# Conv/NSA hybrid decoder step on one core: the compression of the cached blocks in wider and fewer matrix products

## The chip, the cores and the metric

The kernel runs on one core of a Trainium2 chip. The metric is device time in microseconds (us) for one execution; a kernel's time is the median of its runs.

## The reference, cut to what matters

The reference is one inference step of a two-layer decoder, for a prompt of 256 new tokens and for 8 sequences with 4 new tokens each and 2048 cached positions. Nearly all of its arithmetic is in four feed-forward blocks and in the projections of a short convolution and of a sparse attention. The part that the change touches is the compressed branch of the attention: the cached keys and values of each sequence are cut into blocks of 32 positions, and each block is turned into one key and one value by a small two-layer network.

```python
def compress(rows, pe, w1k, w2k, w1v, w2v):
    B, T = rows.shape[:2]
    blk = rows.reshape(B, T // L_CMP, L_CMP, 2, N_KV_HEADS, HEAD_DIM) + pe[:, None, None, :]
    k = jax.nn.gelu(jnp.einsum('bnlkd,lde->bnke', blk[:, :, :, 0], w1k)) @ w2k
    v = jax.nn.gelu(jnp.einsum('bnlkd,lde->bnke', blk[:, :, :, 1], w1v)) @ w2v
    return k, v
```

Here L_CMP is 32, there are 4 key/value heads of 64, and a sequence's 2048 cached positions lie in 16 pages of 128 positions, so in 64 blocks.

## The kernel before, in words

The activations stand with features on the 128 partitions and the 288 tokens (256 + 32) in the free dimension. The large products run as three passes in a rounded 32-bit format: each weight chunk is loaded into a `raw` buffer (four buffers, SyncE's queue, SP), ScalarE (ACT) writes its high part `whi`, VectorE (DVE) its low part `wlo` (lines 227 and 236), and TensorE (PE) multiplies high by high, high by low and low by high, each with 288 columns, all through the helper `mm` (line 292). PE thus runs through the program's products one after the other, and ACT, DVE and POOL prepare weights and take results away beside it.

The compression does not depend on the new tokens. It is written as a generator, `cmp_side` (lines 727 to 799), and `tick` (line 482) takes a step of it now and then while the first three feed-forward blocks and the convolution are put into the program; each `yield` says how much of that work must pass before the next step. So the compression's products stand between the large ones, in PE's one order.

Its work comes in 16 pieces, two for each of the 8 sequences. A piece is 8 whole pages (a `cp` tile of 128 x 8 x 512, two buffers); the page's 512 columns are 2 (key or value) x 16 steps x 16 (4 blocks x 4 heads), and the partitions hold two positions of 64 features. For each of the 16 steps, and for keys and values, one product of a 128 x 64 weight with 128 columns is added into the hidden tile `H` (lines 784 to 786): 32 products, the key's into partitions 0 to 63 and the value's into 64 to 127. They are in plain float32, which PE runs as two instructions each. `gelu_hidden` (line 703) and `gelu_hidden2` (line 711) put the activation on H with ACT, DVE and POOL. `second` (lines 768 to 777) applies the second layer to the hidden tile of the piece before, right behind a piece's 32 products: two products for the keys (weights `W2`, 64 columns each), four for the values (the hidden tile as 64 x 32 weights, `W2` as 64 columns), and two copies out, into `KcT` (DVE) and `Vc` (ACT). In the trace these read as `acc<-cp,W`, `acc<-Hs,W` and `acc<-W,Hs`.

Pages are loaded through SP two pieces ahead, in four groups of two pages for a piece (`load`, line 735): a group reads its page numbers and then gives out one transfer of 256 KB for each page. The weight loads use the same queue, in the order of the program.

Behind these stages come the attention, whose order a planner of costs and ranks (class `Plan`) sets, the output projection and the last feed-forward block. At the planner's end three weight preparations for the output projection (`EARLY`, lines 1485 to 1488) have a rank of about 100; all other ranks lie between -57 and 37, and a lower rank goes first.

Of the kernel before, what the change touches and what calls it, by code (L numbers as in the profile page):

```python
# [8 lines left out]
F32 = mybir.dt.float32  # L9
F32R = mybir.dt.float32r  # L10
I32 = mybir.dt.int32
AF = mybir.ActivationFunctionType
# [4 lines left out]
P = 128  # L17
# [5 lines left out]
NB = 8  # L23
NT = 4
NS = NB * NT
N = NP + NS
KV = 4
# [233 lines left out]
def tile_step(ctx, tc, x_turned, vectors, state_turned, cmp_pages, sel_pages, cache_win, win_pages, page_table,  # L261
# [3 lines left out]
    nc = tc.nc  # L265
# [19 lines left out]
    def trb():  # L285
        return bank("tr")

    def accb():
        return bank("acc")

    def mm(out, lhsT, rhs, start, stop):
        nc.tensor.matmul(out, lhsT, rhs, start=start, stop=stop, skip_group_check=True)  # L292
# [4 lines left out]
    ffn0 = work.enter_context(tc.tile_pool(name="ffn0", bufs=2))  # L297
    pti = const.tile([1, NB * 16], I32, name="pti")
    sT = ffn0.tile([P, KD, 16], F32, name="sT", bufs=1)
    W2 = const.tile([P, HD], F32, name="W2")  # L300
# [20 lines left out]
    def tr(out, in_):  # L321
# [4 lines left out]
    W = Weights(nc, raw, split, RAW, dict(  # L326
        w_ffa_gu=w_ffa_gu, w_ffa_down=w_ffa_down, w_ffb_gu=w_ffb_gu, w_ffb_down=w_ffb_down, w_conv_in=w_conv_in,
        w_conv_out=w_conv_out, w_nsa_in=w_nsa_in, w_nsa_out=w_nsa_out))
# [32 lines left out]
    for _ in range(4):  # L361
        c = W.chunk()
# [47 lines left out]
    def begin(pg, pu):  # L410

        nc.scalar.activation(root, eps, AF.Sqrt)
        warm = accb()
        for n in range(WARM):
            mm(warm[:, :P], ones, ones, True, True)

        def filler(n):
            for _ in range(n):
                mm(warm[:, :P], ones, ones, True, True)

        W.convert()
        for d in range(KD):
            gated_hi(d, V_FFA)
        for d in range(KD):
            gated_lo(d, V_FFA)
        hi, lo = W.take()
        steps = FIRST.split()
        for n, step in enumerate(steps):
            if step == ".":
                filler(2)  # L430
                continue
            k = int(step[1])
            w, x = (lo if step[0] == "l" else hi), (xl if step[0] == "x" else xh)
            mm(pg[:, :N], w[:, k], x[:, k], n == 0, n == len(steps) - 1)
        W.convert()

        sq = []
        room = ffn0.tile([P, 8, 512], F32, name="cp").rearrange("p a c -> p (a c)")[:, :9 * N].rearrange("p (d c) -> p d c", c=N)
        for d in range(0, KD, 3):
            n = min(3, KD - d)  # L440
            sq.append(room[:, d:d + n])
            nc.scalar.activation(sq[-1], xT[:, d:d + n], AF.Square)
            if len(sq) == 1:
                W.convert()
        hi, lo = W.take()
        for w, xs in ((hi, (xh, xl)), (lo, (xh,))):
            for k in range(KD):
                for x in xs:
                    mm(pu[:, :N], w[:, k], x[:, k], k == 0 and w is hi and x is xh, k == KD - 1 and w is lo)
        nc.vector.tensor_add(sq[0], sq[0], sq[1])  # L450
        nc.vector.tensor_add(sq[0][:, :2], sq[0][:, :2], sq[2])
        nc.vector.tensor_add(ss, sq[0][:, 0], sq[0][:, 1])
        nc.vector.tensor_add(ss, ss, sq[0][:, 2])
        load_rest()
# [245 lines left out]
    KcT = mid.tile([P, 2, NB, 64], F32, name="KcT")  # L700
    Vc = mid.tile([P, NB, KV * HD], F32, name="Vc")
    b1 = const.tile([P, 1], F32, name="b1")
    def gelu_hidden(H, w, pool):
        x, x2 = [pool.tile([P, P], F32, name=n)[:, :w] for n in ("Hx", "Hs")]
        nc.scalar.activation(x if len(H.shape) == 2 else x.rearrange("e (k g n) -> e k g n", k=H.shape[1], g=H.shape[2]), H, AF.Identity, bias=b1)
        nc.scalar.activation(x2, x, AF.Square)
        nc.vector.tensor_scalar(x2, x2, 0.044715, 1.0, op0=OP.mult, op1=OP.add)
        nc.gpsimd.tensor_mul(x2, x2, x)
        return x, x2
# [11 lines left out]
    def page_numbers(n, k):  # L721

        return nc.values_load_multi_w_load_instructions(
            pti[0:1, n:n + k], engines=(mybir.EngineType.SP,), min_val=0, max_val=sel_pages.shape[0] - 1,
            skip_runtime_bounds_check_because="the page table's entries are pages of the caches")[1]

    def cmp_side(cw):

        yield WAITS[0] * FILL
        W1 = load_w1(cw)  # L730
        nc.scalar.dma_start(W2, w_cmp2)
        yield WAITS[1] * FILL
        tiles = {}

        def load(n, j):

            if n < 2 * NB:
                if j == 0:
                    tiles[n] = cw.tile([P, 8, 512], F32, name="cp")
                for k, at_ in enumerate(page_numbers(n * 8 + j * 2, 2)):  # L740
                    nc.sync.dma_start(tiles[n][:, j * 2 + k:j * 2 + k + 1], cmp_pages[bass.ds(at_, 1)].rearrange("s p c -> p s c"))

        for n in range(2):
            for j in range(4):
                load(n, j)
                yield WAITS[2] * FILL

        part = []
        for h in range(2):
            t = [cw.tile([P, N], F32, name=x) for x in ("t1", "t2", "s1", "a")]  # L750
            part.append(cw.tile([P, P], F32, name="Hx" if h else "Hs"))
            for q in range(4):
                v = t[q][:, :256].rearrange("p (s e) -> p s e", s=2)
                s0 = 8 * h + 2 * q
                nc.gpsimd.tensor_tensor(v, W1[:, s0:s0 + 2], vecT[:, V_PE + s0:V_PE + s0 + 2, None].to_broadcast([P, 2, P]), op=OP.mult)
                if q:
                    nc.gpsimd.tensor_add(t[0][:, :256], t[0][:, :256], t[q][:, :256])  # L757
            yield WAITS[3] * FILL
            nc.gpsimd.tensor_add(part[h], t[0][:, :P], t[0][:, P:256])
        nc.gpsimd.tensor_add(part[0], part[0], part[1])  # L760
        yield WAITS[3] * FILL
        pb = accb()
        mm(pb[:, 0:1], part[0], ones[:, 0:1], True, True)
        nc.vector.tensor_scalar(b1, pb[:, 0:1], float(D), None, op0=OP.mult)
        yield 0.3

        def second_of(Hs, b, h):
            def second():
                z = accb()
                for kp in range(2):  # L770
                    mm(z[kp * 64:(kp + 1) * 64, 0:64], W2[0:64],
                       Hs[0:64].rearrange("e (pr kp n) -> e kp pr n", pr=2, kp=2)[:, kp], True, True)
                hs = slice(h * 32, (h + 1) * 32)
                for kv in range(KV):
                    mm(z[hs, 64 + kv * 64:128 + kv * 64], Hs[64:, kv * 32:(kv + 1) * 32], W2[64:], True, True)
                nc.vector.tensor_copy(KcT[:, :, b, hs], z[:, 0:64].rearrange("p (a n) -> p a n", a=2))
                nc.scalar.activation(Vc[hs, b], z[hs, 64:320], AF.Copy)
            return second

        second = None  # L780
        for n in range(2 * NB):
            H = accb()
            v = tiles.pop(n).rearrange("p g (c a x) -> p c a g x", c=2, a=16)
            for st in range(16):
                for c in range(2):
                    mm(H[c * 64:(c + 1) * 64, :P], W1[:, st, c * 64:(c + 1) * 64], v[:, c, st], st == 0, st == 15)
            if second:
                second()
            for j in range(4):
                yield 1.15  # L790
                if j == 0:

                    hidden = gelu_hidden(H[:, :P].rearrange("e (g k n) -> e k g n", g=8, k=KV), P, cw)
                load(n + 2, j)
                if j == 2:
                    gelu_hidden2(*hidden)
            second = second_of(hidden[1], *divmod(n, 2))
        second()
        yield 0.6


    def nsa(at):
# [14 lines left out]
        W1 = load_w1(tin)  # L817
# [162 lines left out]
        order = [(i, j, b2) for i, j in chunks for b2 in range(2)]  # L980
        pages, rings = {}, {}
        room = {"raw": 0, "early": 0, "split": 0}
# [103 lines left out]
        for u in range(KD):  # L1086
            pr, g = divmod(u, 4)
            p = mmb()
# [27 lines left out]
        def step(engine, name, put, after=(), slots=(), uses=(), rank=0.0):  # L1116
            return plan.add(engine, TAKES[name], put, after, slots, uses, rank)
# [365 lines left out]
            prompt_unit(*unit)  # L1483
        before = values_of[:PAGES["until"] // 2]
        for n, engine in enumerate(EARLY):
            before = [step("ACT", "whi", W.high, [*before, loads[len(order) + n // 2]], rank=100.0 + n)]
            lower = {"POOL": nc.gpsimd, "DVE": nc.vector}[engine]
            step(engine, "wlo" if engine == "POOL" else "wlo_v", lambda n=W.done + n, lower=lower: W.low(n, lower), before, rank=100.5 + n)

        room["split"] = PAGES["split"]  # L1490
        load_more(0.0)
# [108 lines left out]
```

## Time and profile before

| | us |
|---|---|
| median of 3 runs (1264.59 to 1267.12) | 1266.42 |
| time of the profiled execution | 1265.62 |
| its span, first to last instruction | 1263.5 |
| PE busy in the span | 1242.1 (98%) |
| DVE busy | 719.9 (57%) |
| ACT busy | 582.8 (46%) |
| POOL busy | 250.3 (20%) |
| compression, first layer, PE busy (`acc<-cp,W`) | 59.4 |
| DMA, mean | 207 GB/s |

The span is 2.1 us shorter than the profiled execution's own time, and that time is 0.8 us under the median. In the rows below, PE is the matrix product and PEld the load of its weights; a name such as `acc<-cp,W` is the tile written and the tiles read; `128*64 128x128` is the weight (rows * columns) and the moving operand (partitions x columns). Several products of one kind that run in one another's wake are merged into one row of the timeline: the time from its start to the next row's start is what the group took of PE's time, while the duration of one product holds the filling and emptying of the array too, and so is longer than the distance from one to the next.

### The profile page before, as it was taken

Reading aid. Unit: us, or ns where it says so; the run is one execution under the profiler, and the core shown is the slowest. Engines: PE = TensorE matmul, PEld = TensorE weight load, DVE = VectorE, ACT = ScalarE, POOL = GpSimd, SP = SyncE. Lnnn points to the kernel's source line nnn. Section 1 sums busy time; section 2 is a strip of 40 time slices with the busy share of each in tenths; the row PEclk is TensorE's granted clock in tenths of the full one; section 3 lists DMA queues with packets and bytes.
Section 4 is the critical chain, followed back from the end, with each engine's and each line's share of the span. In section 5 each row is a group of like instructions: output and inputs, shape, how many; then the busy total and the mean of one; then the engine's idle time right before and its main releaser. Section 6 shows DMA issues by size and latency. Waiting matters only on the chain.

```text
span 1263.5 us, 26708 instructions
## 1 busy us (share of the span) xinstructions
PE 1242.1 (98%) x10679; PEld 1193.5 (94%) x10679; DVE 719.9 (57%) x1377; ACT 582.8 (46%) x1054; POOL 250.3 (20%) x261
## 2 busy tenths in 40 slices
PE   9999999999999999999999999999999999999997
PEld 8999999999989999999999999999866599999997
DVE  6653455666655445556464456576568666644553
ACT  6443344533453334345444344544288655443444
POOL 0260121222212101112121022130022122210211
PEclk9999999999999999999999999999999999999999
DMA  7754645656546456546563544487799857565432
GB/s 274 267 199 174 229 162 190 250 184 214 187 159 226 168 202 222 199 155 216 211 227 124 184 144 141 152 302 232 231 359 332 297 213 267 214 249 200 157 104 78
DMA packets 71565, 262.06 MB, mean 207 GB/s; under 512 B 7953, under 2 KB 9874, under 8 KB 56210
## 3 DMA queue, kind: packets, MB, share of 16 engines
q1 hardware_dynamic: 70418, 249.66, 55.7%
q0 software_dynamic: 256, 8.32, 1.7%
q10 hardware_dynamic: 768, 2.38, 0.5%
q8 instruction: 84, 1.38, 0.4%
q14 instruction: 39, 0.32, 0.1%
HBM read 257.31 MB, written 11.35 MB: 213 GB/s over the span
## 4 chain that ended last, share of the span: by engine, by line
PE 88%; ACT 4%; DVE 3%; DMA 2%; POOL 1%; issue 1%; SPq 1%; ACTq 0%; DVEq 0%; POOLq 0%
PE mm L292 78%; PE acc L292 8%; PE tr L323 2%; ACT whi L227 1%; DVE wlo L236 1%; ACT S L1199 1%; SPq L997 1%; ACT L523 1%; DMA early<-in_sel_pages_dram 0%; POOL t L757 0%; DMA raw<-in_w_nsa_out_dram 0%; POOL a L538 0%; ACT sq L385 0%; DMA wlo<-in_sel_pages_dram 0%; DMA raw<-in_w_ffa_gu_dram 0%
## 5 line engine op out<-in xcount | busy, mean ns | idle before, releaser
L292 PE MATMUL mm<-xh,whi 128*128 128x288 f32 x1832 | 544.9, 299 | 3.0 <-DVE xl L1464 1.6
L292 PE MATMUL mm<-xh,wlo 128*128 128x288 f32 x1832 | 540.0, 297 | 0.7 <-DVE wlo L236 0.7
L292 PE MATMUL mm<-xl,whi 128*128 128x288 f32 x1832 | 533.2, 293 | 0.0
L236 DVE TENSOR_TENSOR wlo<-raw,whi 128x1024 fp32r<-128x1024 f32 (+2 forms) x361 | 406.4, 1139 | 120.5 <-ACT whi L227 117.7
L227 ACT ACTIVATE whi<-raw 128x1024 fp32r<-128x1024 f32 (+2 forms) x365 | 343.1, 953 | 90.1 <-PE mm L292 81.2
L292 PEld LDWEIGHTS mm<-xh,whi 128*128 128x128 f32 x1832 | 344.4, 189 | 6.2 <-issue 1.9
L292 PEld LDWEIGHTS mm<-xl,whi 128*128 128x128 f32 x1832 | 346.8, 190 | 0.5 <-DVE xl L379 0.2
L292 PEld LDWEIGHTS mm<-xh,wlo 128*128 128x128 f32 x1832 | 341.9, 187 | 1.8 <-DVE wlo L236 1.6
L292 PE MATMUL mm<-Ah,wlo 128*128 128x288 f32 x768 | 228.5, 297 | 1.7 <-DVE wlo L236 1.7
L292 PE MATMUL mm<-Ah,whi 128*128 128x288 f32 x768 | 228.1, 297 | 1.5 <-ACT Ah L541 1.0
L292 PE MATMUL mm<-Al,whi 128*128 128x288 f32 x768 | 227.3, 296 | 0.4 <-DVE Al L542 0.4
L538 POOL TENSOR_TENSOR a<-s,t 128x288 f32<-128x288 f32 x88 | 115.1, 1307 | 492.6 <-DVE t L536 322.2
L292 PEld LDWEIGHTS mm<-Ah,whi 128*128 128x128 f32 x768 | 145.1, 189 | 2.4 <-ACT Ah L541 1.2
L292 PEld LDWEIGHTS mm<-Ah,wlo 128*128 128x128 f32 x768 | 144.1, 188 | 3.1 <-DVE wlo L236 3.1
L292 PEld LDWEIGHTS mm<-Al,whi 128*128 128x128 f32 x768 | 144.5, 188 | 0.6 <-DVE Al L542 0.6
L541 ACT ACTIVATE Ah<-a 128x288 fp32r<-128x288 f32 x88 | 39.2, 445 | 143.9 <-POOL a L538 143.7
L534 ACT ACTIVATE s<-t 128x288 f32<-128x288 f32 x88 | 39.2, 445 | 141.9 <-DVE t L532 141.7
L536 DVE TENSOR_TENSOR t<-mm,rB 128x288 f32<-128x288 f32 x88 | 40.2, 456 | 90.6 <-PE mm L292 90.5
L542 DVE TENSOR_TENSOR Al<-a,Ah 128x288 fp32r<-128x288 f32 x88 | 40.7, 462 | 68.6 <-ACT Ah L541 68.6
L572 DVE SCALAR_TENSOR_TENSOR xT<-mm,xT 128x288 f32<-128x288 f32 x64 | 29.2, 457 | 83.3 <-PE mm L292 83.2
L292 PE MATMUL acc<-cp,W 128*64 128x128 f32 x1024 | 59.4, 274 | 0.0
L292 PEld LDWEIGHTS acc<-cp,W 128*64 128x64 f32 x1024 | 55.6, 137 | 2.8 <-issue 2.8
(282 smaller groups left out, 870.4 us busy)
## 6 DMA issues: line engine op xcount, KB each, us to landing
raw<-in_w_ffb_gu_dram SPq DMA_DIRECT2D x44, 1024.0 KB
raw<-in_w_ffa_gu_dram SPq DMA_DIRECT2D x42, 1024.0 KB
cp<-in_cmp_pages_dram SPq DMA_DIRECT2D x128, 256.0 KB
early<-in_sel_pages_dram SPq DMA_DIRECT2D x56, 256.0 KB
raw<-in_w_ffa_down_dram SPq DMA_DIRECT2D x16, 768.0 KB
raw<-in_w_conv_in_dram SPq DMA_DIRECT2D x12, 1024.0 KB
raw<-in_w_ffb_down_dram SPq DMA_DIRECT2D x16, 768.0 KB
raw<-in_sel_pages_dram SPq DMA_DIRECT2D x48, 256.0 KB
```

What stands on the lines that cost most here:

```text
L227: self.nc.scalar.activation(parts[0], v, AF.Copy)
L236: (lower or self.nc.vector).tensor_sub(parts[1], v, parts[0])
L292: nc.tensor.matmul(out, lhsT, rhs, start=start, stop=stop, skip_group_check=True)
L323: nc.tensor.transpose(out, in_, ident[:k, :k])
L523: nc.scalar.activation(root, eps, AF.Sqrt)
L534: nc.scalar.activation(s1, t1, AF.Silu)
L536: nc.vector.tensor_mul(t2, pu[:, :N], rB)
L538: nc.gpsimd.tensor_mul(a, s1, t2)
L541: nc.scalar.activation(Ah[:, f], a, AF.Copy)
L542: nc.vector.tensor_sub(Al[:, f], a, Ah[:, f])
L572: nc.vector.scalar_tensor_tensor(xT[:, d], py[:, :N], 0.5, xT[:, d], op0=OP.mult, op1=OP.add)
L997: nc.sync.dma_start(v[:, s:s + 1], sel_pages[bass.ds(at_[s0 + s], 1)].rearrange("s p c -> p s c"))
```

## The change

A piece is now half the steps of all 16 pages of a sequence, where it was all steps of half the pages. The cache's columns are laid out so (16 steps, then key or value) that a page's two halves of 256 columns are 8 steps each; the layout is made outside the timed program, as before. A piece's products are 16, with 256 columns each, and a sequence's two pieces add into the same H, which now comes from the bank ring `tr` and not `acc`. The activation and the second layer run once a sequence, on 256 hidden columns. A page group is now four half pages, each a transfer of 128 KB whose rows are 1 KB. The ranks of the `EARLY` preparations go from about 100 to about 1000.

```diff
-    def gelu_hidden(H, w, pool):
-        x, x2 = [pool.tile([P, P], F32, name=n)[:, :w] for n in ("Hx", "Hs")]
+    def gelu_hidden(H, w, pool, **k):
+        x, x2 = [pool.tile([P, w], F32, name=n, **k) for n in ("Hx", "Hs")]
...
             if n < 2 * NB:
+                b, h = divmod(n, 2)
                 if j == 0:
-                    tiles[n] = cw.tile([P, 8, 512], F32, name="cp")
-                for k, at_ in enumerate(page_numbers(n * 8 + j * 2, 2)):
-                    nc.sync.dma_start(tiles[n][:, j * 2 + k:j * 2 + k + 1], cmp_pages[bass.ds(at_, 1)].rearrange("s p c -> p s c"))
+                    tiles[n] = cw.tile([P, 16, 256], F32, name="cp")
+                for k, at_ in enumerate(page_numbers(b * 16 + j * 4, 4)):
+                    nc.sync.dma_start(tiles[n][:, j * 4 + k:j * 4 + k + 1],
+                                      cmp_pages[bass.ds(at_, 1), :, h * 256:(h + 1) * 256].rearrange("s p c -> p s c"))
...
-        def second_of(Hs, b, h):
-            def second():
-                z = accb()
-                for kp in range(2):
-                    mm(z[kp * 64:(kp + 1) * 64, 0:64], W2[0:64],
-                       Hs[0:64].rearrange("e (pr kp n) -> e kp pr n", pr=2, kp=2)[:, kp], True, True)
-                hs = slice(h * 32, (h + 1) * 32)
-                for kv in range(KV):
-                    mm(z[hs, 64 + kv * 64:128 + kv * 64], Hs[64:, kv * 32:(kv + 1) * 32], W2[64:], True, True)
-                nc.vector.tensor_copy(KcT[:, :, b, hs], z[:, 0:64].rearrange("p (a n) -> p a n", a=2))
-                nc.scalar.activation(Vc[hs, b], z[hs, 64:320], AF.Copy)
-            return second
-
-        second = None
+        def second(Hs, b):
+            z, y = accb(), accb()
+            for kp in range(2):
+                mm(z[kp * 64:(kp + 1) * 64, 0:P], W2[0:64], Hs[0:64].rearrange("e (pr kp n) -> e kp pr n", pr=2, kp=2)[:, kp], True, True)
+            for kv in range(KV):
+                mm(y[0:64, kv * 64:(kv + 1) * 64], Hs[64:, kv * 64:(kv + 1) * 64], W2[64:], True, True)
+            nc.vector.tensor_copy(KcT[:, :, b], z[:, 0:P].rearrange("p (a n) -> p a n", a=2))
+            nc.scalar.activation(Vc[0:64, b], y[0:64, :256], AF.Copy)
+
+        hidden = None
         for n in range(2 * NB):
-            H = accb()
-            v = tiles.pop(n).rearrange("p g (c a x) -> p c a g x", c=2, a=16)
-            for st in range(16):
+            b, h = divmod(n, 2)
+            if h == 0:
+                H = trb()
+            v = tiles.pop(n).rearrange("p g (a c x) -> p a c g x", c=2, a=8)
+            for st in range(8):
                 for c in range(2):
-                    mm(H[c * 64:(c + 1) * 64, :P], W1[:, st, c * 64:(c + 1) * 64], v[:, c, st], st == 0, st == 15)
-            if second:
-                second()
+                    mm(H[c * 64:(c + 1) * 64, :256], W1[:, 8 * h + st, c * 64:(c + 1) * 64], v[:, st, c], h == 0 and st == 0, h == 1 and st == 7)
+            if hidden and h:
+                second(hidden[1], b - 1)
             for j in range(4):
                 yield 1.15
-                if j == 0:
-
-                    hidden = gelu_hidden(H[:, :P].rearrange("e (g k n) -> e k g n", g=8, k=KV), P, cw)
+                if h and j == 0:
+
+                    hidden = gelu_hidden(H[:, :256].rearrange("e (g k n) -> e k g n", g=16, k=KV), 256, cw)
                 load(n + 2, j)
-                if j == 2:
+                if h and j == 2:
                     gelu_hidden2(*hidden)
-            second = second_of(hidden[1], *divmod(n, 2))
-        second()
+        second(hidden[1], NB - 1)
...
-            before = [step("ACT", "whi", W.high, [*before, loads[len(order) + n // 2]], rank=100.0 + n)]
+            before = [step("ACT", "whi", W.high, [*before, loads[len(order) + n // 2]], rank=1000.0 + n)]
...
-            step(engine, "wlo" if engine == "POOL" else "wlo_v", lambda n=W.done + n, lower=lower: W.low(n, lower), before, rank=100.5 + n)
+            step(engine, "wlo" if engine == "POOL" else "wlo_v", lambda n=W.done + n, lower=lower: W.low(n, lower), before, rank=1000.5 + n)
```

On PE, the fourth piece in the program (n = 3, the second one of sequence 1) stands behind a factor's product and ahead of a feed-forward product. The program counts a float32 product once, where the trace shows its two instructions. Before:

```order
L292 MATMUL mm<-xh,wlo 128x288
L292 MATMUL acc<-ss,ones 128x288
L292 MATMUL acc<-cp,W_509 64x128 x32
L292 MATMUL acc<-Hs,W_77 64x64 x2
L292 MATMUL acc<-W_77,Hs 32x64 x4
L292 MATMUL mm<-xh,whi 128x288
```

With the change, in the same place:

```order
L292 MATMUL mm<-xh,wlo 128x288
L292 MATMUL acc<-ss,ones 128x288
L292 MATMUL tr<-cp,W_509 64x256 x16
L292 MATMUL acc<-Hs,W_77 64x128 x2
L292 MATMUL acc<-W_77,Hs 64x64 x4
L292 MATMUL mm<-xh,whi 128x288
```

The fifth piece (n = 4, the first one of sequence 2), which had a second layer behind it too, with the change:

```order
L292 MATMUL mm<-xl,whi 128x288
L292 MATMUL mm<-xh,wlo 128x288
L292 MATMUL tr<-cp,W_509 64x256 x16
L292 MATMUL mm<-xh,whi 128x288
L292 MATMUL mm<-xl,whi 128x288
```

All 16 pieces keep their places between the large products; the second layer stays behind 7 of them and once at the end (16 times before), and nothing else on PE moves.

On SP, two weight loads of the first feed-forward block and the page groups about them, before (`TENSOR_LOAD` reads the page numbers, `ISA` sets an address):

```order
L204 DMA raw<-in_w_ffa_down_dram 128x1280 x2
L723 TENSOR_LOAD pti
L741 ISA
L741 DMA cp<-in_cmp_pages_dram 128x512
L741 ISA
L741 DMA cp<-in_cmp_pages_dram 128x512
L204 DMA raw<-in_w_ffa_down_dram 128x1280 x2
```

With the change, a group of the same stage:

```order
L204 DMA raw<-in_w_ffa_down_dram 128x1280 x2
L723 TENSOR_LOAD pti
L743 ISA
L743 DMA cp<-in_cmp_pages_dram 128x256
L743 ISA
L743 DMA cp<-in_cmp_pages_dram 128x256
L743 ISA
L743 DMA cp<-in_cmp_pages_dram 128x256
L743 ISA
L743 DMA cp<-in_cmp_pages_dram 128x256
L204 DMA raw<-in_w_ffa_down_dram 128x1280
```

There are 64 such groups in both kernels; each has four transfers where it had two, and the weight load behind it stands behind two transfers more.

## Rows read from the trace of the kernel before

**Rows 1.** The page: busy time of the engines, the clock's slices, the chain that ended last.

```profile
PE 1242.1 (98%) x10679; PEld 1193.5 (94%) x10679; DVE 719.9 (57%) x1377; ACT 582.8 (46%) x1054; POOL 250.3 (20%) x261
...
PE 88%; ACT 4%; DVE 3%; DMA 2%; POOL 1%; issue 1%; SPq 1%; ACTq 0%; DVEq 0%; POOLq 0%
```

**Rows 2.** Busy time by engine from the compression's first product to its last.

```profile
core 0: us, PE busy (x) PEld busy (x) DVE busy (x) ACT busy (x) POOL busy (x), PEclk, DMA share, GB/s
109.00:744.00 635.00, 632.57 (x5404) 622.44 (x5403) 342.12 (x529) 269.74 (x427) 120.80 (x133) 1.00 0.55 193
```

**Rows 3.** PE's waits in the same stretch: who waited for whom, total, times, longest.

```profile
PE mm L292 <- DVE wlo L236: 1.9, 4, 0.7
PE mm L292 <- ACT whi L227: 0.5, 1, 0.5
```

**Rows 4.** PE's timeline at the first piece: start, duration, engine, line, product, count.

```profile
109.21 3.71 PE L292 MATMUL acc<-cp,W 128*64 128x128 f32 x64
112.85 0.40 PE L292 MATMUL mm<-Ah,whi 128*128 128x288 f32 x1
```

**Rows 5.** PE's timeline at the fourth piece and its second layer.

```profile
241.93 3.71 PE L292 MATMUL acc<-cp,W 128*64 128x128 f32 x64
245.57 0.33 PE L292 MATMUL acc<-Hs,W 64*64 64x64 f32 x4
245.84 0.63 PE L292 MATMUL acc<-W,Hs 64*32 64x64 f32 x8
246.40 0.40 PE L292 MATMUL mm<-xh,whi 128*128 128x288 f32 x1
```

**Rows 6.** PE's timeline in the attention: products of 64 weight columns with 256 and 128 columns.

```profile
934.72 0.65 PE L292 MATMUL acc<-PA,V 128*64 128x256 f32 x4
935.21 0.39 PE L292 MATMUL acc<-PB,V 128*64 128x128 f32 x4
935.42 0.60 PE L292 MATMUL acc<-PA,V 128*64 128x256 f32 x4
935.86 0.39 PE L292 MATMUL acc<-PB,V 128*64 128x128 f32 x4
```

**Rows 7.** PE's groups by form: products of 64 weight columns with 32 columns; the second layer.

```profile
L292 PE MATMUL acc<-XP,W 128*64 128x32 f32 x64 | 2.1, 223 | 0.0
...
L292 PEld LDWEIGHTS acc<-W,Hs 64*32 64x32 f32 x128 | 7.5, 106 | 1.1
...
L292 PEld LDWEIGHTS acc<-Hs,W 64*64 64x64 f32 x68 | 3.3, 131 | 2.9 <-issue 2.9
```

**Rows 8.** SP's waits in the whole span, longest first: the weight loads', the page groups'.

```profile
SPq L204 <- DVE wlo L236: 630.5, 124, 13.7
SPq L204 <- DVE Al L542: 95.1, 10, 13.6
...
SPq L741 <- PE acc L292: 12.0, 3, 5.7
```

**Rows 9.** SP's timeline: a page group between two weight loads.

```profile
161.62 0.34 SPq L204 DMA_DIRECT2D raw<-in_w_ffa_gu_dram  x1
162.74 0.86 SPq L741 DMA_DIRECT2D cp<-in_cmp_pages_dram  x2
165.57 0.34 SPq L204 DMA_DIRECT2D raw<-in_w_ffa_gu_dram  x1
```

**Rows 10.** The page: SP's DMA queue (packets, MB, share of 16 engines' span).

```profile
q1 hardware_dynamic: 70418, 249.66, 55.7%
```

**Rows 11.** Groups by form: the activation's steps on 128 columns, and the nearest wider ones.

```profile
L705 ACT ACTIVATE Hx<-acc,b 128x128 f32<-128x128 f32 x16 | 5.7, 357 | 0.2
L706 ACT ACTIVATE Hs<-Hx 128x128 f32<-128x128 f32 x16 | 5.0, 312 | 0.5
...
L385 ACT ACTIVATE sq<-xT 128x288 f32<-128x288 f32 x48 | 20.6, 429 | 0.0
```

More of the change, by code (lines that the diff above doesn't have):

```diff
@@ L437, in begin @@
         sq = []
-        room = ffn0.tile([P, 8, 512], F32, name="cp").rearrange("p a c -> p (a c)")[:, :9 * N].rearrange("p (d c) -> p d c", c=N)
+        room = ffn0.tile([P, 16, 256], F32, name="cp").rearrange("p a c -> p (a c)")[:, :9 * N].rearrange("p (d c) -> p d c", c=N)
         for d in range(0, KD, 3):
@@ L750, in cmp_side @@
             t = [cw.tile([P, N], F32, name=x) for x in ("t1", "t2", "s1", "a")]
-            part.append(cw.tile([P, P], F32, name="Hx" if h else "Hs"))
+            part.append(cw.tile([P, 256], F32, name="Hx" if h else "Hs")[:, :P])
             for q in range(4):
@@ L1581 @@
     c = given["cache_cmp_kv"][0].reshape(-1, 4, 16, 2, 2, KV, HD)
-    given["cmp_pages"] = c.transpose(0, 3, 6, 4, 2, 5, 1).reshape(-1, P, 512)
+    given["cmp_pages"] = c.transpose(0, 3, 6, 2, 4, 5, 1).reshape(-1, P, 512)
     given["sel_pages"] = turned(given.pop("cache_sel_kv")[0])
```

## The prediction, on record before the changed kernel ran

> **What bounds the kernel now.** I read the page first. PE is busy for 98% of the span and 88% of the chain that ended last lies on it, against 4% on ACT, 3% on DVE and 2% on transfers [rows 1]. That is an average, so the second view is the busy time in the stretch in which the compression runs, from 109 us to 744 us: PE is busy for 632.57 of 635 us at a granted clock of 1.00 (the 2.4 GHz level), DVE for 54% and ACT for 42% of it, and the transfers hold 0.55 of the DMA engines [rows 2]. The third view is PE's waits there: five, 2.4 us together, all for converted weights and none for a page, a bank or the compression's activation [rows 3]. So in this stretch a microsecond of products that goes away is a microsecond of the kernel, as long as weights and pages come in time. The fourth view, PE's timeline, gives what the compression's products take of that time, read from one row's start to the next row's start.
>
> **First layer.** A piece is 64 instructions (32 products, two passes each) and lasts from 109.21 to 112.85, that is 3.64 us, with the change of form at both ends inside [rows 4]. The key's and the value's products go to different halves of the array and run side by side, so I count pairs: 32 pairs in 3.64 us, 0.114 us each with the ends. After the change a piece is 16 pairs with 256 columns. The attention has just this form, 64 weight columns and 128 or 256 columns in float32, also in pairs: two pairs of 256 columns take 935.86 - 935.42 = 0.44 us, two pairs of 128 columns 935.42 - 935.21 = 0.21 us [rows 6]. So a pair takes 0.22 us with 256 columns and 0.105 us with 128: time goes by columns, and there are as many columns as before. What is left is a few nanoseconds a pair. By the attention's rows 32 x 0.105 = 3.36 us against 16 x 0.22 = 3.52 us, a loss of 0.16 us a piece that is within the timeline's last digit (0.01 us over two pairs); at the other end, if nothing of the 3.64 us were the ends', 3.64 - 3.52 = 0.12 us would be gained. The ends are there, though: the attention's first group of 256 columns, 934.72 to 935.21, is 0.05 us longer than its second, for the new form. I choose a value between, a pair at 0.109 (an estimate, midway from 0.105 to 0.114) and 0.002 saved for each pair of instructions that is no longer there: a gain of 0.05 us a piece, 16 x 0.05 = **0.8 us**, with bounds of -2.6 (16 x 0.16) and +1.9 (16 x 0.12).
>
> Here a rule of the Trainium skill speaks against the rows. "TensorE: Matmul & The Clock Gate", section "What happens when you issue a matmul" (its phase FILL), says that throughput is purely as many cycles as there are columns, one column a cycle, which at 2.4 GHz would be 107 ns for 256 columns; the rows show twice that for float32, and by the rule the present 0.11 us for a pair of 128 columns would be something other than columns. What that would give is the first rival.
>
> **Second layer.** Behind a piece it lasts from 245.57 to 246.40, 0.83 us: 0.27 us for the keys and 0.56 us for the values [rows 5]. There are 16 of them, one after each of 15 pieces and one at the end: 16 x 0.83 = 13.3 us leave PE. Eight come back. The values' part keeps its eight instructions of 64 columns and only takes 64 weight columns instead of 32: I leave it at 0.56. The keys' part has four instructions, in two pairs, with 128 columns instead of 64; a pair of 64 columns costs half of a pair of 128, so the two pairs grow by 2 x 0.055 = 0.11 us, to 0.38. Together 0.94 us, 8 x 0.94 = 7.5 us, and the gain is 13.3 - 7.5 = **5.8 us**. Bounds: if the wider weights of the values show in full, each of the eight instructions grows by 131 - 106 = 25 ns, the difference of the two weight loads [rows 7], 0.2 us a sequence and 1.6 us in all, so a gain of 4.2; if the keys' longer products hide their own change of form, 8 x 0.11 more, a gain of 6.7. That loads of 64 weight columns do not set the pace is seen where 64 columns of weight meet only 32 columns: 64 instructions in 2.1 us, 33 ns each [rows 7], while the eight instructions of the values' part have 70 ns each (0.56 us by eight, with the ends). So I take the first value and keep both bounds.
>
> **What lies beside PE and costs nothing.** The activation's steps and the two copies run eight times and not sixteen, on twice the columns. A step of 288 columns takes ACT 429 ns where 128 columns take 312 to 357 ns [rows 11], so all of them get shorter in sum, but the longest stay on ACT, the two steps in a row that stand ahead of a weight conversion, goes from 0.67 us to at most 0.86 us. What covers it is ACT's idle half [rows 2] and two conversions made ahead; without that cover it would cost 8 x 0.2 = 1.6 us, and as much again on DVE. H stays open over two pieces in a bank ring that nothing else uses there; z and y take both `acc` banks at once, where H and z took them before. The last second layer stands a whole round of steps behind its activation, as before. The ranks of about 1000 change nothing: 100 was already above every other rank, and no row moves in the planner's part on any engine.
>
> **Transfers.** The bytes stay. SP gives out 128 transfers more; a group of two takes 0.86 us of its time [rows 9], so a group of four about 1.75, and a weight load behind one starts up to 0.9 us later. What covers that is that SP sits waiting for a `raw` buffer to come free, 630.5 us over 124 waits, 5 us each [rows 8], and that four `raw` buffers stand ahead of PE. The rows of a transfer are 1 KB and not 2 KB, 16,384 packets more. The trace has no row of such packets alone: at the least they cost nothing beyond their bytes, at the most each costs a whole mean packet, 0.557 x 16 x 1263.5 / 70418 = 0.16 us [rows 10], which over 16 engines and 635 us adds 0.26 to a share of 0.55. That is still under 1. I take zero.
>
> **Sum.** 0.8 + 5.8 = 6.6 us. The profiled execution took 1265.62 us, so 1259.0; the median of the runs stands 0.8 us above that execution, and the forecast for the median is 1266.42 - 6.6 = **1259.8 us**.
>
> **Rivals.**
> 1. *The pairs go by instruction and not by columns.* If 0.11 us were the price of a pair of instructions whatever the columns, as the rule on one column a cycle would have it, a piece would shrink by 16 x 0.11 = 1.75 us, 28 us in all, and the time would be 1259.8 - 27 = 1232.6 (the 0.8 being part of it). Against it stands the pair of 256 columns in [rows 6], twice the pair of 128. Chance 0.02.
> 2. *The gain is spent on waits for weights.* PE's five waits are all for conversions [rows 3]; if the longer stays on ACT and on DVE showed in full, 8 x (0.2 + 0.2) = 3.2 us, and the second layer came to its lower bound, 0.8 + 4.2 - 3.2 = 1.8 us would be left: 1264.6. The lower bounds of both layers together, 4.2 - 2.6 = 1.6, end at 1264.8 as well. For it: PE does wait for both engines now, if rarely. Against it: the sums on both engines fall. Chance 0.08.
> 3. *Slower: pages or weights come late.* A piece's first product waits for 16 transfers where it waited for 8, and each weight load stands behind twice the page transfers. The point from which this decides is 6.6 / 16 = 0.41 us of new wait a piece; if PE had to pay the 0.9 us of SP's time at each of 64 groups it would lose 57 us, and the time would be 1317. Against it: no wait for a page now [rows 3], pages are asked for two pieces ahead, which is some 90 us (three pieces from 109.21 to 241.93 [rows 4, 5]), SP is mostly idle [rows 8]. The Trainium skill's "DMA: Bandwidth & Descriptors", section Bandwidth, advises transfers of 1 MiB or more and shows the rate falling with size, and the change goes the other way; no run here shows the rate of a 128 KB transfer alone. Chance 0.03.
>
> **How the numbers follow.** A measurement of this kernel can tell about 0.2%, 2.5 us, from no change. The forecast's own case has 0.87 and ends 4.5 to 8 us below the median: the bounds of the second layer, 4.2 and 6.7, with the first layer's +0.8, a little more or less PE waiting, and a run-to-run spread of 1 us. The range of 1257.5 to 1262.8 holds that case without its last tails; beyond it lie rival 1 below, rivals 2 and 3 above. Faster by over 0.2%: the forecast's case, less a hundredth for its upper tail, and rival 1, 0.88. Within 0.2%: rival 2 and that tail, 0.09. Slower: 0.03.
>
> **What would show it.** In the profile after, right: 512 instructions `tr<-cp,W` of 256 columns whose pieces last 3.55 to 3.65 us from start to next start; a second layer of 0.9 to 1.0 us behind every second piece and nothing behind the others; PE's busy time in the stretch about 6.5 us less and its waits still near 2.4 us; a DMA share between 0.55 and 0.6. Wrong: pieces near 1.9 us (rival 1); waits of PE for ACT or DVE of 5 us or more (rival 2); a first product of a piece that waits for `cp`, or ACT waiting for `raw` (rival 3). The forecast fails in size if the values' products with 64 weight columns take over 80 ns each.

## The result, and the profile after

The changed kernel takes 1254.6 us (median of six runs, 1254.24 to 1256.68); the kernel before, run beside it, 1266.12 us (six runs, 1263.93 to 1267.12). The ratio is 0.9914, 95% interval 0.9904 to 0.9924. The forecast was 1259.8 with a range of 1257.5 to 1262.8: the direction held, the gain is larger than the range allowed. The execution profiled now took 1254.44 us with a span of 1252.7, the one before 1265.62 with 1263.5: 11.2 us to explain.

The page of the kernel after, the lines that answer to [rows 1, 10]:

```profile
PE 1231.4 (98%) x10071; PEld 1165.2 (93%) x10071; DVE 718.8 (57%) x1353; ACT 574.7 (46%) x1022; POOL 248.8 (20%) x245
...
q1 hardware_dynamic: 88850, 249.67, 57.2%
...
PE 88%; ACT 4%; DVE 3%; POOL 2%; DMA 1%; issue 1%; SPq 0%; ACTq 0%; DVEq 0%; POOLq 0%
```

The bound is the same: PE is 98% busy, with 10.7 us less busy time. The windows view over the same stretch as [rows 2] (us, busy time and count of PE, PEld, DVE, ACT, POOL, then granted clock, DMA share, GB/s), and below it the waits of PE from 109 to 736 us, which answer to [rows 3]:

```profile
109.00:744.00 635.00, 632.48 (x4858) 604.35 (x4858) 346.84 (x513) 266.02 (x402) 120.13 (x118) 1.00 0.57 196
```

```profile
PE mm L292 <- DVE wlo L236: 1.9, 4, 0.7
PE mm L292 <- ACT whi L227: 0.5, 1, 0.5
```

PE's sum in the window looks unchanged because the compression now ends 8 us earlier, at about 736 us, and other products fill the rest of the window: a fixed window on the engine that bounds shows no gain, only an earlier end of the work does. The waits in this view are the same five as before, 2.4 us, none for a page; four pauses of PE too short for it stand in the table below. The DMA share went from 0.55 to 0.57. SP's timeline shows a page group between two weight loads (start, duration, queue, line, transfer, count), against [rows 9]:

```profile
160.57 0.34 SPq L204 DMA_DIRECT2D raw<-in_w_ffa_gu_dram  x1
161.52 1.92 SPq L743 DMA_DIRECT2D cp<-in_cmp_pages_dram  x4
164.75 0.34 SPq L204 DMA_DIRECT2D raw<-in_w_ffa_gu_dram  x1
```

Four transfers take SP 1.92 us where two took 0.86, about what the prediction put (1.75; the next group, at 165.64 us, takes 2.72), and PE has no wait for a page in this stretch.

PE's timeline of the kernel after, at the fourth piece and its second layer, against [rows 5]:

```profile
239.94 3.67 PE L292 MATMUL tr<-cp,W 128*64 128x256 f32 x32
243.55 0.33 PE L292 MATMUL acc<-Hs,W 64*64 64x128 f32 x2
243.56 0.32 PE L292 MATMUL acc<-W,Hs 64*64 64x64 f32 x2
243.71 0.28 PE L292 MATMUL acc<-Hs,W 64*64 64x128 f32 x2
243.73 0.51 PE L292 MATMUL acc<-W,Hs 64*64 64x64 f32 x6
244.17 0.40 PE L292 MATMUL mm<-xh,whi 128*128 128x288 f32 x1
```

A piece lasts 3.60 us from start to next start (3.64 before): the first layer is as forecast. The second layer lasts from 243.55 to 244.17, 0.62 us, and not the 0.94 of the forecast. The rows show how: the keys' products (`Hs,W`, 128 columns) and the values' (`W,Hs`, 64 columns) alternate in time, 243.55, 243.56, 243.71, 243.73. In [rows 5] all keys' products came first and the values' followed.

Where the 11.2 us came from, by the start of the same product in the two traces:

| stretch | gain, us | what it is |
|---|---|---|
| before the first piece | 0.2 | it starts at 108.99 and not 109.21; other runs have 108.9 to 109.7 |
| first layer | 0.6 | 16 x (3.645 - 3.604) |
| second layer | 8.2 | 16 x 0.822 - 8 x 0.619 |
| 299 to 362 us | -0.65 | PE pauses for `wlo` four times for 0.05 to 0.23 us, twice before |
| to 1012 us | 0.9 | 0.3 at a wait for an `early` page (1.5 to 1.2 us), 0.57 at a weight load of `w_nsa_out` (5.43 to 4.87 us); two executions of one and the same kernel differ by 1.2 us here, so this need not be the change's |
| 1012 to 1016 us | 1.5 | a drop of the granted clock that only the profile before has |
| outside the span | 0.3 | 2.07 to 1.75 us; over all runs of the two kernels 2.07 to 1.88 |

Two of these needed experiments: why the second layer is so short, and whether the clock belongs to the change.

### The profile page after: what moved, and what is told of

Same layout as the page of the kernel before. It is cut to its first block, busy times and chain, and to the rows that moved or that the text cites. A ratio compares the mean times of both kernels' runs of the same rounds, so it can differ in the third digit from the quotient of the medians.

```text
span 1252.7 us, 25849 instructions
## 1 busy us (share of the span) xinstructions
PE 1231.4 (98%) x10071; PEld 1165.2 (93%) x10071; DVE 718.8 (57%) x1353; ACT 574.7 (46%) x1022; POOL 248.8 (20%) x245
## 4 chain that ended last, share of the span: by engine, by line
PE 88%; ACT 4%; DVE 3%; POOL 2%; DMA 1%; issue 1%; SPq 0%; ACTq 0%; DVEq 0%; POOLq 0%
PE mm L292 79%; PE tr L292 5%; PE acc L292 3%; PE tr L323 2%; DVE wlo L236 1%; ACT whi L227 1%; ACT S L1199 1%; ACT L523 1%; POOL t L760 0%; DMA early<-in_sel_pages_dram 0%; POOL a L538 0%; DMA raw<-in_w_nsa_out_dram 0%; ACT sq L385 0%; DMA raw<-in_w_ffa_gu_dram 0%; SPq L997 0%
## 5 line engine op out<-in xcount | busy, mean ns | idle before, releaser
L538 POOL TENSOR_TENSOR a<-s,t 128x288 f32<-128x288 f32 x88 | 119.9, 1362 | 544.4 <-DVE t L536 430.8
L292 PE MATMUL tr<-cp,W 128*64 128x256 f32 x512 | 58.8, 382 | 0.0
L376 ACT ACTIVATE xh<-xT,vecT 128x288 fp32r<-128x288 f32 x48 | 25.1, 534 | 64.4 <-DVE xT L572 38.6
```

The lines of the kernel that those rows point to most:

```text
L376: nc.scalar.activation(normed[0][:, d], xT[:, d], AF.Copy, scale=vecT[:, v + d:v + d + 1])
L538: nc.gpsimd.tensor_mul(a, s1, t2)
```

## The experiments

**Is it the shape or the bank that made the second layer short?** The change did two things to it. The values' weights became 64 columns wide, so that keys (array rows 0 to 63) and values (rows 64 to 127) both have tiles of 64 x 64, where the values had 64 x 32. And keys and values write two banks, `z` and `y`, where they shared one. A bank is one of the areas that PE writes its results to. Theory A is the shape, theory B the bank. The first experiment keeps the changed kernel's two banks and takes the shape back:

```diff
-                mm(y[0:64, kv * 64:(kv + 1) * 64], Hs[64:, kv * 64:(kv + 1) * 64], W2[64:], True, True)
+                for a in range(2):
+                    mm(y[a * 32:(a + 1) * 32, kv * 64:(kv + 1) * 64], Hs[64:, kv * 64 + a * 32:kv * 64 + (a + 1) * 32], W2[64:], True, True)
```

> The changed kernel with the values' second layer in products of 32 weight columns again, two side by side (16 program products a sequence in place of 4; y keeps its own bank). Theory A, shape: in the changed kernel the second layer lasts 0.62 us and not 0.94 because keys and values have the same 64 x 64 shape on different rows of the array and so run side by side; with 64 x 32 they no longer do, and a second layer lasts about 0.95 us, 8 x 0.33 = 2.6 us in all: 1257.2 us. Theory B, bank: they run side by side because z and y lie in different banks; a second layer stays at 0.6 to 0.65 us and the time at 1254.6 us.

It took 1259.23 us (1258.56 to 1260.43), ratio to before 0.9952 [0.9936, 0.9968]. Its timeline of PE:

```profile
244.21 0.44 PE L292 MATMUL acc<-Hs,W 64*64 64x128 f32 x4
244.58 0.64 PE L292 MATMUL acc<-W,Hs 64*32 64x64 f32 x16
245.15 0.40 PE L292 MATMUL mm<-xh,whi 128*128 128x288 f32 x1
```

In two banks the 64 x 32 products come behind the 64 x 64 ones again, and the second layer lasts 0.94 us. That is the number of the forecast, in the form that the forecast had in mind. Two banks alone, theory B, do not put them side by side. The time is 2.0 us over theory A's 1257.2, and rose by more than the layer's 8 x 0.315 = 2.5 us (3.3 us against the runs of the changed kernel with the same mean clock); 0.7 us of the difference stand in its trace ahead of the layers, and its profile has the drop of the clock that is treated below.

The second experiment does the reverse: the kernel before, with two banks and its own shapes.

```diff
-                z = accb()
+                z, y = accb(), accb()
...
-                    mm(z[hs, 64 + kv * 64:128 + kv * 64], Hs[64:, kv * 32:(kv + 1) * 32], W2[64:], True, True)
+                    mm(y[hs, 64 + kv * 64:128 + kv * 64], Hs[64:, kv * 32:(kv + 1) * 32], W2[64:], True, True)
...
-                nc.scalar.activation(Vc[hs, b], z[hs, 64:320], AF.Copy)
+                nc.scalar.activation(Vc[hs, b], y[hs, 64:320], AF.Copy)
...
-            H = accb()
+            H = trb()
```

> The kernel before with one edit in the second layer: keys and values go to two banks (H moves to the tr ring to make room), all shapes as before (64 x 64 and 64 x 32). Theory A, shape: nothing runs side by side, a second layer still lasts 0.82 us, and the time is that of the kernel before, 1266.1 us. Theory B, bank: a second layer shrinks to about 0.55 us, 16 x 0.27 = 4.3 us in all: 1261.8 us.

1265.55 us (1263.83 to 1267.06, ten runs), ratio 0.9999 [0.9990, 1.0008]. Its timeline of PE at the fourth piece:

```profile
245.50 0.33 PE L292 MATMUL acc<-Hs,W 64*64 64x64 f32 x4
245.76 0.63 PE L292 MATMUL acc<-W,Hs 64*32 64x64 f32 x8
246.32 0.40 PE L292 MATMUL mm<-xh,whi 128*128 128x288 f32 x1
```

0.82 us, as in [rows 5]. Two banks alone bring nothing here either. So the equal shape is needed. Keys and values of one shape in one bank weren't tried: whether the two banks are needed beside it stays open. The trace before holds one more case, the attention's scores, products of 64 x 128 weights on the two halves of the array's rows, with a bank for each half:

```profile
916.79 1.14 PE L292 MATMUL mm<-kT,qT 64*128 64x256 f32 x8
917.85 0.33 PE L323 MATMUL tr<-ident,S 128*128 128x128 f32 x1
```

These eight take 1.06 us, in pairs whose halves start 7 ns apart (917.324 and 917.331 us) and which follow each other 0.21 to 0.22 us apart once they run; one after the other the eight would take some 1.7 us (8 x 0.21, an estimate from these starts).

**What is the first layer worth by itself?** The changed kernel with the pieces and transfers of the kernel before, and its second layer still once a sequence:

```diff
-                    tiles[n] = cw.tile([P, 16, 256], F32, name="cp")
...
+                    tiles[n] = cw.tile([P, 8, 512], F32, name="cp")
...
-            for st in range(8):
+            v = tiles.pop(n).rearrange("p g (a c x) -> p a c g x", c=2, a=16)
+            for st in range(16):
                 for c in range(2):
-                    mm(H[c * 64:(c + 1) * 64, :256], W1[:, 8 * h + st, c * 64:(c + 1) * 64], v[:, st, c], h == 0 and st == 0, h == 1 and st == 7)
+                    mm(H[c * 64:(c + 1) * 64, h * P:(h + 1) * P], W1[:, st, c * 64:(c + 1) * 64], v[:, st, c], st == 0, st == 15)
```

> The second-layer part of the change alone: pieces of 8 whole pages, 32 products of 128 columns, transfers of 256 KB as before, but H, activation and second layer once a sequence. Theory: the wide first layer is worth 0.04 us a piece, 0.6 us in all, and the smaller transfers nothing, so 1255.2 us with pieces of 3.64 us and second layers of 0.62 us. Rival: the wide pieces or their transfers carry the 2.3 us that the two traces differ by behind the compression; then 1257 to 1258 us.

1257.55 us (1256.78 to 1258.35), ratio 0.9939 [0.9924, 0.9954]. Its timeline of PE:

```profile
240.17 3.71 PE L292 MATMUL tr<-cp,W 128*64 128x128 f32 x64
243.81 0.33 PE L292 MATMUL acc<-Hs,W 64*64 64x128 f32 x2
```

The piece is 3.64 us again, the second layer still 0.62. By the start of the same products its trace is 7.7 us ahead of the kernel before at 855 us, the changed kernel's 8.5. Of these 0.8 us, 0.1 lie ahead of the first piece (it starts at 109.11 and not 108.99), so the wider products are worth 16 x 0.04 = 0.6. The median, 1257.55, is in the rival's range of 1257 to 1258. But all four runs have the lower mean clock, and the profile has the clock's drop; against the changed kernel's runs of the same mean clock (1256.3, below) they are 1.2 us slower, which a spread of about 1 us does not tell from 0.6. That the wide pieces carry the 2.3 us behind the compression does not hold either: 0.8 of them are in this trace as well, and for the other 1.5 a kernel with wide pieces that has the drop stands below. So "sixteen pages in two pieces of eight steps" bears less than a tenth of the gain; "its second layer runs once a sequence" bears the rest.

**Does the clock belong to the change?** This is the windows view of the kernel before, around the last stage, with the columns as above (the granted clock is the third number from the end), then the same place in the kernel after, which comes 9 us earlier:

```profile
1008.00:1012.00 4.00, 1.50 (x42) 1.08 (x34) 1.61 (x6) 1.54 (x5) 0.21 (x1) 1.00 1.01 426
1012.00:1016.00 4.00, 3.86 (x17) 3.86 (x18) 3.28 (x3) 2.78 (x3) 2.16 (x1) 0.57 1.01 426
1016.00:1020.00 4.00, 4.00 (x32) 4.00 (x31) 1.97 (x3) 0.08 (x1) 0.00 (x0) 1.00 0.95 352
```

```profile
999.00:1003.00 4.00, 1.93 (x44) 1.51 (x44) 1.84 (x6) 2.10 (x5) 0.56 (x1) 1.00 0.95 338
1003.00:1007.00 4.00, 4.00 (x31) 4.00 (x31) 3.34 (x2) 2.41 (x3) 1.83 (x1) 1.00 1.00 403
```

Before, PE is busy for 1.50 of 4 us, and then runs 3.41 us at 1.2 GHz instead of 2.4: 17 products in the window where the kernel after has 31. PE's timeline before, with the idle time ahead of a row in brackets, shows the gaps:

```profile
1010.18 0.41 PE L292 MATMUL acc<-Sel,rms 128*128 128x64 f32 x2 [1.08 <-DVE rms L1452]
1012.14 1.16 PE L292 MATMUL mm<-xh,whi 128*128 128x288 f32 x4 [1.55 <-DVE xl L1464]
```

Theory: the drop is a matter of chance that both kernels have, and belongs to neither. Rival: the changed kernel keeps the clock. Both kernels were run again without an edit.

> The kernel before once more, for the spread of its runs with the mean granted clock beside each. Theory: its runs fall in two kinds, about 1264 us at a mean clock of 0.998 or more, and 1265.5 to 1267 us at 0.996 to 0.997, where a drop of 3.4 us to half the clock falls behind the attention; the drop costs about 1.5 us of the 11.5. Rival: the runs do not go by the clock, and the 2.3 us behind the compression belong to the change itself.

The kernel before: 1265.30 us (1262.76 to 1266.85, twelve runs), 0.9997 [0.9989, 1.0006] against the runs beside it. Its profile has the drop once more, 3.41 us at 1012.8. Over the 50 runs of the kernel before in the later comparisons, 36 have a mean granted clock of 0.997 or less and take about 1265.7 us, and 14 have 0.998 or more and take about 1263.7. (The mean also moves with the half clock at the very end, so the divider is not exact: one of the twelve has 0.998 and 1265.08.) The drop alone costs 1.5 us in the trace; the two kinds of runs differ by 2.1, and where the rest comes from was not tried.

> The changed kernel once more, for the spread of its runs with the mean granted clock beside each. Theory: the change itself is worth 9.3 us (runs of a clock of 0.998 against such runs, 1254.4 against 1263.7), and the 11.5 us between the first medians had 2 us from the clock: how many runs hold a drop is chance, so about as many as of the kernel before (26 of 35) hold one, and the median rises to about 1256 us. Rival: the changed kernel keeps the clock more often by itself (4 of the first 6 runs), and the median stays near 1254.5 us.

The changed kernel: 1256.15 us (1254.01 to 1256.49, five runs), ratio 0.9932 [0.9918, 0.9946]. Three of the five have the lower clock, with a mean of 1256.3, and two the higher, 1254.7; in the first comparison two of six had 1256.3 and four 1254.4. So the median of 1254.5 that the rival named did not come again: by the mean clock 5 of 11 runs have the lower clock, against 36 of 50. Whether the changed kernel has the drop more rarely can't be told from so few runs. Its own two profiles have none. The third experiment's profile has it, and so has that of the kernel with the values side by side (the last part below), which has the wide pieces of the changed kernel; one window of each, in this order:

```profile
1004.50:1008.50 4.00, 4.00 (x21) 4.00 (x20) 4.00 (x3) 2.00 (x2) 1.16 (x1) 0.57 0.97 399
1002.00:1006.00 4.00, 4.00 (x21) 4.00 (x20) 4.00 (x3) 2.00 (x2) 1.25 (x1) 0.57 1.00 420
```

Like against like, the change is worth 1265.7 - 1256.3 = 9.4 us, or 1263.65 - 1254.55 = 9.1 (all six runs of the higher clock); the rest of the 11.5 us between the first medians is which kind of run each median fell on.

The length of the second gap does not settle it alone. With no products added, the drop follows gaps of 1.55, 1.73 and 1.17 us (the two profiles of the kernel before and the third experiment), 1.07 (values side by side) and 0.82 (the first experiment); it does not follow 1.02 (the second experiment), 0.99 and 0.83 (the changed kernel).

Then the gaps as the cause: four products of constants into a bank that nobody reads, ahead of the last `turn_out` product, and four behind it, in the kernel before.

```diff
             def turn_out():
+                turned_out.append(i)
+                x = trb() if len(turned_out) == 4 else None
                 t["o"] = accb()
+                for _ in range(4 if x is not None else 0):
+                    mm(x[:, :P], ones, ones, True, True)
                 mm(t["o"][:, :64], t["a"], Sel, True, True)
+                for _ in range(4 if x is not None else 0):
+                    mm(x[:, :P], ones, ones, True, True)
```

> The kernel before with eight products of constants at the attention's end (four ahead of the last turn of an output, four behind it, into a bank that nobody reads), where PE has its idle time of 1.1 and 1.6 us ahead of the output projection. Theory: that idle time is what lets the clock fall to half for 3.4 us behind it, so the drop is gone from nearly all runs, and the median is that of the runs at 0.998, 1263.7 us, while the order of all other work stays. Rival: the drop is settled by other work (the transposes and narrow products of the whole attention); then about three runs in four keep it and the median stays at 1265.5 us.

1263.89 us (1263.36 to 1265.75, eleven runs), ratio 0.9994 [0.9985, 1.0003]. The interval takes in no change, as it must where only some of the runs of the kernel before have the drop; but nine of the eleven runs are at 1264.2 or less, against five of fifteen beside them (a sixth has 1264.23). The count goes by time, because the mean clock does not sort these runs: the profiled one has 0.997 and no drop here, but a longer half clock at the very end. The windows of this kernel, and its timeline of PE in the gap:

```profile
1008.00:1012.00 4.00, 3.65 (x58) 3.06 (x58) 1.78 (x6) 1.71 (x5) 0.26 (x1) 1.00 1.08 401
1012.00:1016.00 4.00, 3.82 (x29) 3.85 (x30) 3.28 (x3) 2.73 (x3) 2.13 (x1) 1.00 0.91 358
```

```profile
1009.15 1.16 PE L292 MATMUL tr<-ones 128*128 128x128 f32 x8
1010.30 0.41 PE L292 MATMUL acc<-Sel,rms 128*128 128x64 f32 x2
1010.54 1.11 PE L292 MATMUL tr<-ones 128*128 128x128 f32 x8
1012.18 1.04 PE L292 MATMUL mm<-xh,whi 128*128 128x288 f32 x6 [0.53 <-DVE xl L1470]
```

PE is busy for 3.65 us where it was for 1.50, the clock stays at 1.00, and 29 products follow where 17 did. The one profile supports the theory, and the count of runs does; the ratio alone would not.

**Can the second layer be shorter still?** If products of one shape go side by side on the two halves of the rows, the two halves of the columns should carry the values two at a time as well. In the changed kernel:

```diff
-            for kv in range(KV):
-                mm(y[0:64, kv * 64:(kv + 1) * 64], Hs[64:, kv * 64:(kv + 1) * 64], W2[64:], True, True)
+            for kv in (0, 2, 1, 3):
+                mm(y[kv // 2 * 64:kv // 2 * 64 + 64, kv % 2 * 64:kv % 2 * 64 + 64], Hs[64:, kv * 64:(kv + 1) * 64], W2[64:], True, True)
...
-            nc.scalar.activation(Vc[0:64, b], y[0:64, :256], AF.Copy)
+            for a in range(2):
+                nc.scalar.activation(Vc[0:64, b, a * P:(a + 1) * P], y[a * 64:(a + 1) * 64, :P], AF.Copy)
```

> The changed kernel with the values' four second-layer products in two halves of the array (heads 0 and 1 to partitions 0 to 63, heads 2 and 3 to 64 to 127, issued in turn), and one copy more out of the bank. Shape theory: products of one shape run side by side on different columns of the array as well as on different rows, so the values' part takes four steps of 58 ns and not eight, a second layer 0.42 us and not 0.62, 1.6 us in all: 1252.8 us at a clock of 0.998. Rival: eight products keep their distance, and the time does not move.

1254.55 us (1253.89 to 1255.86), ratio 0.9922 [0.9907, 0.9937]. Its timeline of PE:

```profile
243.83 0.33 PE L292 MATMUL acc<-Hs,W 64*64 64x128 f32 x2
243.85 0.33 PE L292 MATMUL acc<-W,Hs 64*64 64x64 f32 x4
243.99 0.28 PE L292 MATMUL acc<-Hs,W 64*64 64x128 f32 x2
244.01 0.28 PE L292 MATMUL acc<-W,Hs 64*64 64x64 f32 x4
244.23 0.40 PE L292 MATMUL mm<-xh,whi 128*128 128x288 f32 x1
```

The tail of six values' products is gone: 0.40 us where the changed kernel has 0.62. All four runs have the lower mean clock, and are 1.6 us below the changed kernel's runs of that kind (1254.7 against 1256.3), as expected. Here products of one shape run side by side in one bank, `y`, but on different columns of the array and so in different partitions of the bank. Both edits together:

> Both edits on the changed kernel: the values side by side, and the eight products of constants at the attention's end. If both theories hold, 1252.8 us in nearly every run.

1253.82 us (1252.47 to 1254.66, five runs), ratio 0.9914 [0.9901, 0.9928], with no drop in its profile. That is 1.0 us above the expected 1252.8, which one run of five reaches; why was not tried. It is the fastest version of this study, 2.3 us below the changed kernel beside it by the medians.

## Why the prediction was right in kind and wrong in size

- **What bounds** was right. Every microsecond of products taken out of the compression came through, but for the 0.65 us between 299 and 362 us.
- **First layer**, forecast 0.8 us: 0.64 us by the pieces, in the trace after and again in the third experiment's. Time goes by columns (in the trace after, pairs of 256 columns start 209 ns apart, in the trace before pairs of 128 start 102 to 103), and rival 1 (by instruction, 1.9 us a piece) is ruled out by 3.60.
- **Second layer**, forecast 5.8 us: 8.2 us. This is the step that failed, and in it one clause, "Together 0.94 us". Both parts were sized well: the keys' part alone lasts 0.37 us in the first experiment's timeline (forecast 0.38), and the values' products follow each other every 58 ns in the trace (56 before, 70 in the forecast with the ends), well under the 80 ns that the prediction named as its own failing point. The mistake was to add them. The prediction counted the key's and the value's products of the first layer as pairs, because they lie on different halves of the array, and did not ask the same of the second layer, where they also do. The second layer's own rows gave no sign, since there the shapes differed and the two did follow each other; but the change's line `y[0:64, ...]` gave the values the shape that the keys have, and the trace before holds products of one shape on the two halves of the rows (the attention's scores, shown above), which the prediction did not read. 8 x (0.94 - 0.62) = 2.6 us were missed, and the upper bound of 6.7 did not hold them.
- **Activation steps on ACT, DVE and POOL**, forecast nothing: the waits of [rows 3] are unchanged, so that holds in the main. The 0.65 us given back between 299 and 362 us are short pauses of PE for `wlo` in the convolution's end, which is rival 2 at a fifth of its 3.2 us. One of them, at 335.6 us, is for a conversion right behind an activation step, which took 1.65 us there and 1.41 before. The third experiment, with the old pieces and transfers, has the same four pauses (PE goes on at 323.15, 336.10, 339.59 and 343.06 us), so the transfers are not their cause; that the activation steps are was not tried.
- **Transfers**, forecast nothing: right, with no wait for a page in the compression's stretch and a share of 0.57 in a range of 0.55 to 0.6. The queue took 18,432 packets more, where the prediction counted 16,384. Rival 3 did not come.
- **The clock** had no term. Runs of both kernels with the lower mean clock are about 2 us slower, of which the 3.41 us at half clock take 1.5 in the trace. The profile before had the drop, and so, by its time, had the median of the kernel before; the median of the changed kernel had not, which is luck of the draw. Between runs of one kind the change would have come to 1266.4 - 9.4 = 1257.0 or 1266.4 - 9.1 = 1257.3, still below the range: the second layer's term is what failed, and the clock made it look worse.

## What to carry to other kernels

When a change alters the shape of small products, ask anew which of them may run side by side, and put the time of those that may nearer to the longer part than to the sum (0.62 us here, for parts of 0.37 and 0.56): equal tiles on different rows of the array did overlap here, with a bank for each, and unequal ones did not, in one bank or in two. And where a kernel has a short stretch with gaps on PE, look at the granted clock of several runs behind it before a difference of 0.1% is given to an edit.

## What the runs showed of the hardware

Products of 64 x 64 tiles on array rows 0 to 63 and 64 to 127 start 7 ns apart (243.556 and 243.563 us in the trace after). When the shape goes from 64 x 64 to 64 x 32, the next product starts 148 ns after the last of the old shape, and the one after it 80 ns later, before a pace of 56 ns is reached (the trace before, from 245.687 us). The first two experiments show that two banks do not change this. The Trainium skill, "TensorE: Matmul & The Clock Gate", section "Packing small matmuls — row/col tiling", has products on different row groups start about 4 ns behind each other. The 7 ns of equal shapes come near that; the 148 ns of unequal ones do not, and for them the measurement decides.

Gaps of 1.08 and 1.55 us on PE were followed by 3.41 us at 1.2 GHz, and so were gaps of 1.08 and 0.82 us, while gaps of 1.08 and 1.02 us were not. With eight products in the gaps no drop followed, in one profile of the kernel before and in one of the changed kernel with the values side by side. The time outside the span fell from 2.07 to 1.88 us on average over the runs of the two kernels (1.79 in the first six of the changed one, 2.00 in the other five), with 859 instructions fewer in the traces; its cause was not tried.
